# Convolution's closing norms moved into other buffers, three of its output products held back, and a feed-forward tile finished one product later

## The chip, the cores and the metric

One core of one Trainium2 chip runs the whole kernel. The metric is the device time of one launch in microseconds (us). The engines are TensorE (PE), VectorE (DVE), ScalarE (ACT), GpSimd (POOL) and SyncE (SP); each works through its own instructions in their fixed order, and an instruction that waits holds up all that stand behind it on that engine. DMA transfers are issued from the queue of an engine.

## The reference, cut to what matters

One layer of a decoder trunk runs on 528 prompt tokens (16 of them learned meta tokens) and on 8 sequences of 4 new tokens, each with 4096 cached positions in pages:

```python
h = x + 0.5 * swiglu(rmsnorm(x, ffn1_norm), ...)            # FF = 2816
n = rmsnorm(h, mix_norm)                                    # D = 1024
q_lat, q_rope, c_kv, k_rope, glu = project_mixers(n, ...)
a = attn_fn(q_lat, q_rope, c_kv, k_rope, w_uv)              # 8 heads, 512 wide
cv, conv_state = conformer_conv(glu, conv_prev, ...)        # 512 channels, 31 taps, LayerNorm, silu
mix = concatenate([rmsnorm(a, attn_grp_norm), rmsnorm(cv, conv_grp_norm)]) @ w_out
h = h + mix
h = h + 0.5 * swiglu(rmsnorm(h, ffn2_norm), ...)
```

All data are float32. A product is made of three one-pass products: every operand is split into a high and a low part.

## The kernel before

**Layout.** Channels lie on partitions and tokens along the free dimension, so a product of 128 output channels is a pair of PSUM tiles of half the tokens each. `mm3` (L367) issues, per block of 128 input channels, six matmuls of 272 or 280 columns.

**Stages.** The first feed-forward (`ffn`, L729) works through 22 tiles in `GROUPS` (8, 7, 7). The first `plain` tiles (5 in the first feed-forward, 4 in the second) use ordinary products; the others use seven products of blocks for eight (`seven_unit`, L676), whose operands `Combos` (L621) makes beside the plain tiles. Then comes the projection of the mixers, next to which the sample attention (`sample_proc`, L1143), the convolution (`conv_proc`, L914) and the prompt attention (`prompt_worker`, L1327) run. After them come 16 output products: eight of the convolution's half and eight of the attention's half (`out_half`, L1579), each of which is added to the residual `h` by two DVE additions at L1587. The second feed-forward follows.

**Order.** The order of the program is written by processes that yield estimates of PE time to a small planner (`run`, L408). Of the processes that are ready the one with the lowest number goes first: the sample attention and the norms have 0, the two prompt workers 2, the main process with the products 5. Constants such as `CN_LAT` or `AN_LAT` (L45 to L67) are the latencies that the processes sleep for. The compiler's scheduler then sets the order on each engine from this program and from when buffers come free in its own model.

**Weights.** `w_dma` (L271) loads a block of 128x512 into `wr` (3 buffers) from the queue of SP; `w_split` (L289) copies it to `wh` on ACT (L302) and subtracts to `wl` on POOL (L304), or on DVE for the tiles in `prepared`. In the stages of the mixers the load of block j+2 follows the split of block j, and takes the buffer of block j-1, which that block's subtraction on POOL must have read.

**Pages.** `load_chunk` (L1021) loads a chunk of the cache, eight DMAs of 256 KB each from SP's queue; 32 chunks in all. A chunk has four tiles with the tag "y" (8 buffers) or "w" (4 buffers; every third chunk up to chunk `LAST_W` = 30). `chunk_pv` (L1089) of chunk `LAST_W` sets `w_free`. The main process waits for `conv_done` and for `w_free` (L1589, L1590), loads the residual back into the "w" buffers (L1593), and then starts the output products.

**The convolution's end.** `conv_tail` (L964) subtracts the mean (L971), squares the four channel blocks (L542, tag "t" of the pool `tmp`, 10 buffers, which the prompt workers use for their probabilities and their transposes), sums the squares over channels with small matmuls (L453), takes the reciprocal root (`rsqrt` L448: the root on ACT at L485, the rest on DVE), scales, applies tanh (L986, tag "t" too), squares again, takes the second norm, scales (L905) and splits into high and low (L910 on ACT, L911 on POOL).

**The attention's norm.** `attn_norm` (L1565) waits for both prompt workers and the sample attention, squares the attention's output (L542), sums, takes the root, scales (L905) and splits (L910, L911 on DVE). The attention's eight products wait for it.

**The handover in a feed-forward.** When the last plain tile is done, its `evict` (L772) multiplies the four PSUM halves by the norm (L185), applies Silu (L778), multiplies, and splits; then the first `seven_unit` starts. It snapshots its PSUM tiles on ACT (L695). The last three splits of `Combos` (`last`, L672, at L635 on DVE) stand in the last quarter of that plain tile.

Of the kernel before, what the change touches and what calls it, by code (L numbers as in the profile page):

```python
# [50 lines left out]
US_LAT = 4.96  # L51
UP_LAT = 0.5
CS_LAT = 1.73
CN_LAT = 8.16
AN_LAT = 3.71
TAP_PACE = 1.05
CN_WAIT = 8.0
# [8 lines left out]
PAGE_LAT = 2.04  # L66
WEIGHT_TIME = 0.0  # L67

LAST_W = 30


STEPS = "q0k1plr23ue4567"
# [39 lines left out]
def kernel(  # L112
# [45 lines left out]
    def Tm(shape=None, name="t"):  # L158
        return tmp.tile(shape or [128, T], F32, tag="t", bufs=10, name=name)
# [111 lines left out]
    def w_dma(upto):  # L271
        while st["dma"] < min(upto, len(subs)):
            i, c0, n = subs[st["dma"]]
            if n == 0:
                if c0 == 0:
                    raws[i, "a"] = []
                    for kh in range(2):
                        t = U("y" if i in first_new else "x", [128, 2, 512], F32, "ra")
                        nc.sync.dma_start(out=t, in_=stream[i][0][:, 1024 * kh:1024 * kh + 1024])
                        raws[i, "a"].append(t)  # L280
                st["dma"] += 1
                continue
            t = wpool.tile([128, n], F32, tag="wr", bufs=3, name="wr")
            nc.sync.dma_start(out=t, in_=stream[i][0][:, c0:c0 + n])
            raws[st["dma"]] = t
            dma_free[0] = max(dma_free[0], clock[0]) + n * WEIGHT_TIME
            st["dma"] += 1

    def w_split(upto):  # L289
        while st["split"] < min(upto, len(subs)):  # L290
            j = st["split"]
            n = subs[j][2]
            w_dma(j + 1)
            if n == 0:
                splits[j] = seven(*subs[j][0:2])
                st["split"] += 1
                w_dma(j + 8)
                continue
            raw = raws.pop(j)
            hi = wpool.tile([128, n], F32R, tag="wh", bufs=3, name="wh")  # L300
            lo = wpool.tile([128, n], F32R, tag="wl", bufs=3, name="wl")
            nc.scalar.activation(out=hi, in_=raw, func=AF.Copy)  # L302
            eng = nc.vector if subs[j][0] in prepared else nc.gpsimd
            last_lo[0] = eng.tensor_tensor(out=lo, in0=raw, in1=hi.bitcast(F32), op=ALU.subtract)  # L304
            splits[j] = (hi, lo)
            st["split"] += 1

            w_dma(j + (3 if subs[j][0] in mixers else 4))

    def seven(i, m):  # L310
# [134 lines left out]
    last_sum = [None]  # L445
    last_lo = [None]

    def rsqrt(ssums, oi, q, t0=0, site=0, scale=1.0, times=1.0):  # L448

        p1 = SS([128, q], "p1", "nr")  # L450
        for i, ssum in enumerate(ssums):
            for j in range(4):
                nc.tensor.matmul(  # L453
                    out=p1[32 * j:32 * j + 32, :], lhsT=ones_c[:, 0:32], rhs=ssum[:, t0 + q * j:t0 + q * j + q],
                    start=(i == 0), stop=(i == len(ssums) - 1), tile_position=(0, 32 * j),
                )
        scale *= (0.5, 2.0, 1.0)[oi]
        r = tmp.tile([128, 3, q], F32, tag="r", bufs=1, name="r")
        r0, r1, rx = (r[:, i] for i in range(3))
        if times != 1.0:  # L460
            newton3(p1, r0, r1, rx, scale, times)
        else:
            newton(p1, r0, r1, scale)

        nc.vector.tensor_copy(out=r1.bitcast(F32R), in_=r0)
        rr = tmp.tile([128, q], F32R, tag="rr", bufs=1, name="rr")
        last_rsqrt[0] = nc.vector.scalar_tensor_tensor(out=rr, in0=r1, scalar=lowm[:, 0:1], in1=r0, op0=ALU.mult, op1=ALU.add)
        return rr
# [68 lines left out]
        spawn(norm(), 0)  # L537
        return ev

    def square(part, after=None):  # L540
        sq = Tm([128, part.shape[-1]], "sq")
        behind(nc.scalar.activation(out=sq, in_=part, func=AF.Square), after)  # L542
        return sq

# [184 lines left out]
    def ffn(xs, hook, tail=None, plain=NF):  # L729
        ev = Evict(xs.ev, 1)  # L730
        n = xs.n // 2
        cb = steps = None
        f_all = 0

        while turn[0] != "mm" or turn[-1] == "mm":
            turn.append(turn.pop(0))
        for gi, nf in enumerate(GROUPS):
            hid = []
            for f in range(nf):
                f_all += 1  # L740
                if f_all > plain:
                    yield from ev.drain()
                    xs.x = None
                    yield from seven_unit(Weights(), cb, n, hid)
                    continue
                gu = []
                w = Weights()
                pair = [MF()]
                for kh in range(2):
                    for j in range(2):  # L750
                        if len(pair) == j:
                            yield from ev.room()
                            pair.append(MF())
                        for k in range(4 * kh, 4 * kh + 4):
                            mm3(pair[j], *w.at(1024 * kh + 512 * j + 128 * (k % 4)), xs.x[k][:, 0], xs.x[k][:, 1], n,
                                k == 0, k == KD - 1)
                            yield 0.715
                            ev.flush()
                            if plain < NF and xs.ev.ready:
                                if cb is None:  # L760
                                    cb = Combos(xs)
                                    steps = cb.steps()
                                if k % 3 < 2 and (step := next(steps, None)) is not None:
                                    step()
                                if f_all == plain and kh == 1 and j == 1 and k < 7:
                                    cb.last(k - 3, "x")
                        w.done(1024 * kh + 512 * j)
                    if f_all == plain:
                        for k in range(4 * kh, 4 * kh + 4):
                            xs.x[k] = None  # L770

                def evict(pair=pair, gu=gu, w=w):  # L772
                    for j in range(2):
                        t = Tm([128, 2 * n], "gu")
                        halves(lambda *a: behind(v_mul(*a), last_sum[0] if w.i + 1 in first_new else None),
                               t, pair[j], xs.ev.val, n=n)
                        if j == 0:
                            last_silu[0] = nc.scalar.activation(out=t, in_=t, func=AF.Silu)  # L778
                        gu.append(t)
                    x = U("y", [128, 2, 2 * n], F32R, "hid")  # L780
                    hv = Tm([128, 2 * n], "hv")
                    nc.vector.tensor_tensor(out=hv, in0=gu[0], in1=gu[1], op=ALU.mult)
                    nc.scalar.activation(out=x[:, 0], in_=hv, func=AF.Copy)
                    eng = nc.vector if w.i in prepared else nc.gpsimd
                    eng.tensor_tensor(out=x[:, 1], in0=hv, in1=x[:, 0].bitcast(F32), op=ALU.subtract)
                    hid.append(x)
                ev.add(evict)
            yield from ev.drain()
            if gi == len(GROUPS) - 1:
                xs.x = cb = None  # L790
# [173 lines left out]
    def conv_tail():  # L964
# [7 lines left out]
            yield 0.48  # L972
            yield Sleep(1.5)
        csum[0] = None
        s = [square(acc(ct)) for ct in range(4)]
        yield Sleep(CN_LAT)
        ev = Ev()
        yield from rsqrt_proc(lambda: s, 2, ev, site=4)
        s = []
        yield Sleep(1.0)  # L980
        for ct in range(4):
            a = acc(ct)
            nc.vector.scalar_tensor_tensor(out=a, in0=a, scalar=col(P_LG + ct), in1=ev.val, op0=ALU.mult, op1=ALU.mult)

            t = Tm([128, NQ], "th")
            nc.scalar.activation(out=t, in_=a, func=AF.Tanh, scale=0.5, bias=hlb[:, ct:ct + 1])  # L986
            nc.vector.tensor_scalar(out=a, in0=a, scalar1=col(P_LB + ct), scalar2=None, op0=ALU.add)
            nc.vector.scalar_tensor_tensor(out=a, in0=t, scalar=1.0, in1=a, op0=ALU.add, op1=ALU.mult)
            s.append(square(a))
            yield Sleep(0.8)  # L990
        yield Sleep(CN_LAT)
        ev = Ev()
        yield from rsqrt_proc(lambda: s, 2, ev, site=5, scale=0.25, times=0.5)
        s = None
        yield Sleep(1.0)
        for ct in range(4):
            t = scaled(acc(ct), P_CG + ct, ev.val, Tm([128, NQ], "cg"))
            if ct % 2 == 1:
                acc2[ct // 2] = None
            conv_out[ct] = split(t, nc.gpsimd, "x" if ct == 2 else "z")  # L1000
            yield Sleep(0.8)
        conv_done.set(None, 2.0)

# [341 lines left out]
    def main():  # L1345
# [245 lines left out]
        for j in range(4):  # L1591
            hs[j] = U("w", [128, 2, NQ], F32, "h")
            nc.sync.dma_start(out=hs[j], in_=hscr[:, 2 * j:2 * j + 2, :])  # L1593
        for d in range(KD):
            yield from out_half(conv_out)
        yield a_ev
        f2 = Split(P_F2, NQ)
# [211 lines left out]
```

## Time and profile before

| | |
|---|---|
| median of 3 runs | 1177.47 us (1176.39 to 1177.81) |
| the profiled execution | 1183.17 us |
| its span on the core | 1181.4 us |
| PE busy | 1129.1 us, 96% of the span |
| DVE, ACT, POOL busy | 780.1, 537.2, 333.8 us |

A row of a timeline gives the start and the duration in us, the engine and line, the operation, what it writes and reads, how many instructions are merged, and in brackets how long the engine had been idle and what released it. A busy PE is not PE at its peak: the ends of matmuls are modelled. `PEclk` is the granted clock of TensorE as a share of 2.4 GHz.

### The profile page before, as it was taken

To read this page: it belongs to the slowest core of one execution; us is meant where nothing else is said; L and a number is where in the kernel's file an instruction comes from. 1 tells how busy PE (TensorE), PEld (TensorE's weight loads), DVE (VectorE), ACT (ScalarE), POOL (GpSimd) and SP (SyncE) were. 2 spreads that over 40 slices of the span, in tenths; PEclk is the share of its full clock that TensorE was granted. 3 is DMA by queue.
4 is the path that set the end of the run, shared out by engine and by line. 5 is a ranking of instruction groups with operands and counts; after the bars stand their busy time and mean duration, and the time that the engine had idled before them with its cause. 6 is when DMAs were issued, how large, how long until landed. Compare 5 with 4: busy or idle time off the path is not lost.

```text
span 1181.4 us, 24527 instructions
## 1 busy us (share of the span) xinstructions
PE 1129.1 (96%) x9312; PEld 1029.9 (87%) x9312; DVE 780.1 (66%) x1566; ACT 537.2 (45%) x1120; POOL 333.8 (28%) x344
## 2 busy tenths in 40 slices
PE   8999999999999999998899988899999999999995
PEld 8999999999999987876555546899899999999995
DVE  5987158825884447989777357469881489258834
ACT  5545235523555314533544446255552356235642
POOL 4101310042004645676434402342014100410060
PEclk9999999999999989999889999899999999999998
DMA  5243323232226647989779972223333232323222
GB/s 170 68 156 99 85 67 106 85 117 81 92 72 212 220 149 240 272 285 287 220 236 371 351 237 77 72 89 105 102 116 99 72 100 86 115 77 105 70 70 77
DMA packets 91062, 168.60 MB, mean 143 GB/s; under 512 B 18976, under 2 KB 25120, under 8 KB 90944
## 3 DMA queue, kind: packets, MB, share of 16 engines
q1 hardware_dynamic: 88352, 162.27, 42.8%
q0 software_dynamic: 2048, 4.20, 1.2%
q8 instruction: 74, 1.21, 0.4%
q10 hardware_dynamic: 544, 0.56, 0.1%
q14 instruction: 44, 0.36, 0.1%
HBM read 161.33 MB, written 5.65 MB: 141 GB/s over the span
## 4 chain that ended last, share of the span: by engine, by line
PE 83%; DVE 8%; ACT 3%; DMA 2%; issue 2%; POOL 1%; SPq 0%; DVEq 0%; ACTq 0%; POOLq 0%
PE mm L371 40%; PE mm L688 31%; PE sc L1075 3%; PE ob L1097 2%; DVE cacc L947 2%; PE po L1322 2%; PE s L1266 1%; PE mm L1639 1%; PE pt L1306 1%; DMA out<-glu 1%; DMA page<-in_pool_c 1%; DVE xc L635 1%; DMA wr<-in_f_gu 1%; DVE wl L319 1%; DMA wr<-in_w_out_t 0%
## 5 line engine op out<-in xcount | busy, mean ns | idle before, releaser
L304 POOL TENSOR_TENSOR wl<-wr,wh 128x512 fp32r<-128x512 f32 (+1 forms) x157 | 198.2, 1266 | 653.6 <-ACT wh L302 589.6
L688 PE MATMUL mm<-xc,wh 128*128 128x272 f32 (+1 forms) x1960 | 373.8, 291 | 3.4 <-ACT sn L695 3.3
L688 PEld LDWEIGHTS mm<-xc,wh 128*128 128x128 f32 x1960 | 307.8, 189 | 4.5 <-ACT sn L695 3.7
L688 PE MATMUL mm<-xc,wl 128*128 128x272 f32 (+1 forms) x980 | 282.0, 293 | 0.8 <-DVE wl L319 0.8
L371 PE MATMUL mm<-hid,wh 128*128 128x280 f32 (+1 forms) x1352 | 226.7, 289 | 0.0
L302 ACT ACTIVATE wh<-wr 128x512 fp32r<-128x512 f32 (+1 forms) x177 | 108.0, 612 | 260.4 <-PE mm L371 195.8
L371 PEld LDWEIGHTS mm<-hid,wh 128*128 128x128 f32 x1352 | 192.5, 188 | 0.0
L688 PEld LDWEIGHTS mm<-xc,wl 128*128 128x128 f32 x980 | 183.0, 189 | 6.7 <-DVE wl L319 6.7
L371 PE MATMUL mm<-xs,wh 128*128 128x280 f32 (+2 forms) x992 | 176.4, 298 | 4.1 <-ACT wh L302 1.5
L371 PEld LDWEIGHTS mm<-xs,wh 128*128 128x128 f32 (+1 forms) x992 | 146.5, 192 | 8.5 <-issue 2.7
L812 DVE SCALAR_TENSOR_TENSOR h<-mm,h 128x280 f32<-128x280 f32 (+1 forms) x92 | 36.8, 441 | 162.1 <-PE mm L371 162.1
L371 PE MATMUL mm<-hid,wl 128*128 128x280 f32 (+1 forms) x676 | 141.1, 290 | 0.0
L317 ACT ACTIVATE wh<-ra 128x512 fp32r<-128x512 f32 x140 | 87.9, 630 | 71.9 <-PE mm L688 61.8
L371 PE MATMUL mm<-xs,wl 128*128 128x280 f32 (+2 forms) x496 | 111.4, 299 | 2.6 <-POOL glu L888 1.7
L371 PEld LDWEIGHTS mm<-hid,wl 128*128 128x128 f32 x676 | 106.4, 188 | 0.0
L317 ACT ACTIVATE wh<-ws 128x512 fp32r<-128x512 f32 x105 | 66.2, 630 | 83.8 <-DVE ws L329 44.1
L319 DVE TENSOR_TENSOR wl<-ra,wh 128x512 fp32r<-128x512 f32 x140 | 96.3, 689 | 5.6 <-ACT wh L317 2.4
L319 DVE TENSOR_TENSOR wl<-ws,wh 128x512 fp32r<-128x512 f32 x105 | 72.5, 691 | 28.6 <-ACT wh L317 25.8
L947 DVE SCALAR_TENSOR_TENSOR cacc<-glu,par,cacc 128x512 f32<-128x512 f32 x120 | 89.8, 749 | 1.3
L371 PEld LDWEIGHTS mm<-xs,wl 128*128 128x128 f32 (+1 forms) x496 | 80.9, 191 | 6.2 <-issue 2.3
L1028 POOL DMA_INDIRECT rope<-in_pool_r,pr_sb x64 | 63.5, 991 | 54.0 <-PE sc L1075 41.9
L695 ACT ACTIVATE sn<-mm 128x272 f32<-128x272 f32 (+1 forms) x105 | 40.7, 389 | 27.4 <-PE mm L688 27.3
(252 smaller groups left out, 1499.0 us busy)
## 6 DMA issues: line engine op xcount, KB each, us to landing
page<-in_pool_c SPq DMA_DIRECT2D x256, 256.0 KB, 5.3
ra<-in_f_gu SPq DMA_DIRECT2D x70, 512.0 KB, 4.0
wr<-in_f_d SPq DMA_DIRECT2D x62, 256.0 KB, 2.7
wr<-in_f_gu SPq DMA_DIRECT2D x36, 256.0 KB, 3.0
wr<-in_w_in_t SPq DMA_DIRECT2D x24, 256.0 KB, 5.3
wr<-in_f_d SPq DMA_DIRECT2D x30, 192.0 KB, 2.4
wr<-in_w_out_t SPq DMA_DIRECT2D x16, 256.0 KB, 3.0
h<-in_x_t SPq DMA_DIRECT2D x8, 280.0 KB, 6.5
```

The lines of the kernel that those rows point to most:

```text
L302: nc.scalar.activation(out=hi, in_=raw, func=AF.Copy)
L304: last_lo[0] = eng.tensor_tensor(out=lo, in0=raw, in1=hi.bitcast(F32), op=ALU.subtract)
L317: nc.scalar.activation(out=hi, in_=w, func=AF.Copy)
L319: ins = nc.vector.tensor_tensor(out=lo, in0=w, in1=hi.bitcast(F32), op=ALU.subtract)
L371: nc.tensor.matmul(out=ps[a][:m, 0:n], lhsT=w, rhs=x[:, a * n:(a + 1) * n], start=first and o == 0 and j == 0, stop=last and o == 1,)
L688: nc.tensor.matmul(out=ps, lhsT=w_[:, c], rhs=x, start=first and k == 0 and j == 0, stop=k == 3 and j == 2, skip_group_check=True)
L695: nc.scalar.activation(out=s, in_=src, func=AF.Copy)
L812: last = halves(lambda o, i, x: nc.vector.scalar_tensor_tensor(out=o, in0=i, scalar=0.5, in1=x, op0=ALU.mult, op1=ALU.add), hk(d), ps, hk( ...
L947: last_tap = nc.vector.scalar_tensor_tensor(out=ps, in0=g[:, tp:S0 + tp], scalar=w, in1=ps, op0=ALU.mult, op1=ALU.add)
L1028: last = nc.gpsimd.indirect_dma_start(out=rope[:, pg], out_offset=None, in_=pool_r, in_offset=bass.IndirectOffsetOnAxis(ap=pr_sb[:, 32 * g ...
L1075: nc.tensor.matmul(out=ps[32 * b:32 * b + 32], lhsT=w[:, g, 32 * b:32 * b + 32], rhs=x, start=(i_ == 0), stop=(i_ == 2), tile_position=(0, ...
L1097: nc.tensor.matmul(out=ob[32 * b:32 * b + 32, :], lhsT=pts[:, 128 * pg + 32 * b:128 * pg + 32 * b + 32], rhs=tiles[b][:, pg, 0:256], start ...
```

## The change

1. `conv_tail` squares into buffers with the tag "g" (4 buffers, the convolution's own) and issues the sums of each block right behind its square, into a PSUM tile that it holds; tanh goes to "g" as well and is squared in place; the last scaling is in place, without a tile "t". Two of the four outputs take buffers "x" in place of one.
2. `w_dma` issues the weights of the mixers (projections, latents and output, 49 blocks) from ACT's queue.
3. `LAST_W` goes from 30 to 27: chunk 30 takes "y" buffers, and the "w" buffers are free after chunk 27.
4. Before the convolution's sixth output product (`HELD` = 5) the main process waits for the prompt workers and the sample attention, so that three products are left for the time of the attention's norm.
5. In both feed-forwards the `evict` of the last plain tile follows the first product (and a quarter of the second) of the first `seven_unit`; two of the last splits of `Combos` come about a quarter of a tile earlier, the third behind that `evict`. An order that held the `evict` behind the sums of the block weights is dropped.

```diff
-CN_LAT = 8.16
+SQ_LAT = 1.2
+SW_LAT = 3.4
-LAST_W = 30
+LAST_W = 27
+HELD = 5
...
-            nc.sync.dma_start(out=t, in_=stream[i][0][:, c0:c0 + n])
+            (nc.scalar if i in mixers else nc.sync).dma_start(out=t, in_=stream[i][0][:, c0:c0 + n])
...
-                    yield from seven_unit(Weights(), cb, n, hid)
+                    unit = seven_unit(Weights(), cb, n, hid)
+                    if held:
+                        for _ in range(5):
+                            yield next(unit)
+                        held.pop()()
+                        cb.last(3, "x")
+                    yield from unit
...
-                                if f_all == plain and kh == 1 and j == 1 and k < 7:
-                                    cb.last(k - 3, "x")
+                                if f_all == plain and kh == 1 and j == 0 and k in (5, 6):
+                                    cb.last(k - 4, "x")
...
-                        halves(lambda *a: behind(v_mul(*a), last_sum[0] if w.i + 1 in first_new else None),
-                               t, pair[j], xs.ev.val, n=n)
+                        halves(v_mul, t, pair[j], xs.ev.val, n=n)
...
-                ev.add(evict)
+                if f_all == plain < NF:
+                    held.append(evict)
+                else:
+                    ev.add(evict)
...
-        s = [square(acc(ct)) for ct in range(4)]
-        yield Sleep(CN_LAT)
+        p1 = SS([128, NQ // 4], "p1", "nr")
+        for ct in range(4):
+            sq = square(acc(ct), None, "g")
+            yield Sleep(SQ_LAT)
+            column_sums(p1, sq, NQ // 4, ct == 0, ct == 3)
+            sq = None
+            yield 0.25
         ev = Ev()
-        yield from rsqrt_proc(lambda: s, 2, ev, site=4)
+        yield from rsqrt_proc(lambda: p1, 2, ev, site=4)
...
-            t = Tm([128, NQ], "th")
+            t = U("g", [128, NQ], F32, "th")
...
-            s.append(square(a))
-            yield Sleep(0.8)
-        yield Sleep(CN_LAT)
+            nc.scalar.activation(out=t, in_=a, func=AF.Square)
+            yield Sleep(SW_LAT)
+            column_sums(p1, t, NQ // 4, ct == 0, ct == 3)
+            t = None
+            yield 0.25
...
-            t = scaled(acc(ct), P_CG + ct, ev.val, Tm([128, NQ], "cg"))
+            conv_out[ct] = split(scaled(acc(ct), P_CG + ct, ev.val), nc.gpsimd, "x" if ct in (1, 2) else "z")
...
         for d in range(KD):
+            if d == HELD:
+                for e in p_done + [s_done]:
+                    yield e
             yield from out_half(conv_out)
```

`column_sums` holds the four matmuls that stood in `rsqrt`, which now also takes a PSUM tile that is already summed.

## Rows read from the trace of the kernel before

**Rows 1.** Busy engines and the chain that ended last, from the page.

```profile
PE 1129.1 (96%) x9312; PEld 1029.9 (87%) x9312; DVE 780.1 (66%) x1566; ACT 537.2 (45%) x1120; POOL 333.8 (28%) x344
PE 83%; DVE 8%; ACT 3%; DMA 2%; issue 2%; POOL 1%; SPq 0%; DVEq 0%; ACTq 0%; POOLq 0%
```

**Rows 2.** Windows: us, busy of each engine (count), granted clock, DMA share, GB/s.

```profile
641.00:685.00 44.00, 39.56 (x446) 23.16 (x448) 21.35 (x90) 24.79 (x83) 17.65 (x32) 1.00 0.94 330
685.00:728.00 43.00, 40.30 (x465) 23.18 (x460) 25.38 (x88) 22.83 (x74) 3.12 (x10) 0.96 0.56 193
728.00:748.00 20.00, 13.34 (x92) 12.11 (x85) 16.96 (x26) 8.73 (x15) 9.26 (x6) 0.83 0.08 27
748.00:788.00 40.00, 40.00 (x322) 40.00 (x321) 20.56 (x40) 17.64 (x28) 17.70 (x14) 1.00 0.27 85
...
836.00:860.00 24.00, 21.02 (x149) 20.01 (x148) 20.88 (x37) 11.67 (x23) 0.00 (x0) 0.93 0.17 56
```

**Rows 3.** The convolution's end by line, 560 to 790 us (mean, squares, second scaling).

```profile
L971 DVE TENSOR_TENSOR acc<-acc,mu x8: 429/430/438, 637.8 to 640.3; 128x272 f32<-128x272 f32 x8
L542 ACT ACTIVATE sq<-acc x8: 650/666/674, 669.1 to 715.8; 128x544 f32<-128x544 f32 x8
L905 DVE SCALAR_TENSOR_TENSOR cg<-acc,par,rb x4: 779/783/1864, 727.3 to 729.4; 128x544 f32<-128x544 f32 x4
```

**Rows 4.** Timeline, 724 to 757 us: the attention's norm and the first output products.

```profile
727.13 0.66 ACT L542 ACTIVATE sq<-at 128x544 f32<-128x544 f32 x1
727.20 1.14 PE L453 MATMUL p<-sq,ones_c 128*32 128x136 f32 x32 [0.42 <-DVE rb L508]
730.17 1.28 ACT L485 ACT_TABLE_LOAD   x1
731.87 1.00 DVE L486 RECIPROCAL r<-r 128x136 f32<-128x136 f32 x1 [0.63 <-ACT r L485]
732.99 0.30 DVE L487 SCALAR_TENSOR_TENSOR r<-p,r 128x136 f32<-128x136 f32 x1
733.96 1.34 DVE L489 SCALAR_TENSOR_TENSOR r<-r 128x136 f32<-128x136 f32 x1
737.03 4.91 DVE L905 SCALAR_TENSOR_TENSOR at<-at,par,rb 128x544 f32<-128x544 f32 x4
742.35 0.82 PE L371 MATMUL mm<-mix,wh 128*128 128x272 f32 x2 [4.04 <-DVE h L1587]
743.26 2.62 DVE L911 TENSOR_TENSOR mix<-at,mix 128x544 fp32r<-128x544 f32 x4
753.70 0.79 DVE L1587 TENSOR_TENSOR h<-mm,h 128x272 f32<-128x272 f32 x2 [2.22 <-PE mm L371]
756.72 0.79 DVE L1587 TENSOR_TENSOR h<-mm,h 128x272 f32<-128x272 f32 x2 [2.23 <-PE mm L371]
```

**Rows 5.** All additions to the residual behind the output products, by line.

```profile
L1587 DVE TENSOR_TENSOR h<-mm,h x32: 424/431/442, 741.9 to 787.9; 128x272 f32<-128x272 f32 x32
```

**Rows 6.** Timeline, 680 to 686 us: the stall behind the first norm's root.

```profile
684.64 1.07 PE L1097 MATMUL ob<-page,pts 128*32 128x256 f32 x16 [3.21 <-ACT pts L1086]
```

**Rows 7.** Timelines at the two handovers: 79 to 82 us and 836 to 846 us.

```profile
81.75 0.53 PE L688 MATMUL mm<-xc,wh 128*128 128x280 f32 x2 [0.78 <-ACT sn L695]
...
841.57 0.67 ACT L695 ACTIVATE sn<-mm 128x272 f32<-128x272 f32 x2
842.00 0.52 PE L688 MATMUL mm<-xc,wh 128*128 128x272 f32 x2 [2.49 <-ACT sn L695]
```

**Rows 8.** Timelines near 580 and 1171 us: a weight block that lands late; a DMA issued from ACT.

```profile
581.33 0.63 ACT L302 ACTIVATE wh<-wr 128x512 fp32r<-128x512 f32 x1 [4.11 <-DMA wr<-in_w_out_t]
582.65 1.08 PE L1075 MATMUL sc<-rope,qbd 128*32 128x256 f32 x8 [4.28 <-ACT pts L1086]
...
1170.71 0.42 ACTq L1664 DMA_DIRECT2D out<-y  x1
```

**Rows 9.** Waits of SP's queue, 400 to 770 us: us in total, times, longest.

```profile
SPq L284 <- POOL wl L304: 80.4, 20, 27.3
```

More of the change, by code (lines that the diff above doesn't have):

```diff
@@ L446, with column_sums @@
     last_lo = [None]
-    def rsqrt(ssums, oi, q, t0=0, site=0, scale=1.0, times=1.0):
[L450 to L456, printed above, removed]
+    def column_sums(p1, ssum, q, first, last, t0=0):
+        for j in range(4):
+            nc.tensor.matmul(
+                out=p1[32 * j:32 * j + 32, :], lhsT=ones_c[:, 0:32], rhs=ssum[:, t0 + q * j:t0 + q * j + q],
+                start=first, stop=last, tile_position=(0, 32 * j),
+            )
+    def rsqrt(ssums, oi, q, t0=0, site=0, scale=1.0, times=1.0):
+        if isinstance(ssums, list):
+            p1 = SS([128, q], "p1", "nr")
+            for i, ssum in enumerate(ssums):
+                column_sums(p1, ssum, q, i == 0, i == len(ssums) - 1, t0)
+        else:
+            p1 = ssums
         scale *= (0.5, 2.0, 1.0)[oi]
@@ L538, in rsqrt_after, with square @@
         return ev
-    def square(part, after=None):
-        sq = Tm([128, part.shape[-1]], "sq")
+    def square(part, after=None, home="t"):
+        sq = Tm([128, part.shape[-1]], "sq") if home == "t" else U(home, [128, part.shape[-1]], F32, "sq")
         behind(nc.scalar.activation(out=sq, in_=part, func=AF.Square), after)
@@ L732, in ffn @@
         cb = steps = None
+        held = []
         f_all = 0
@@ L786, in evict @@
                     hid.append(x)
-                ev.add(evict)
+                if f_all == plain < NF:
+                    held.append(evict)
+                else:
+                    ev.add(evict)
             yield from ev.drain()
@@ L974, in conv_tail @@
         csum[0] = None
-        s = [square(acc(ct)) for ct in range(4)]
-        yield Sleep(CN_LAT)
+        p1 = SS([128, NQ // 4], "p1", "nr")
[5 more added lines that the diff above has]
+            yield 0.25
         ev = Ev()
-        yield from rsqrt_proc(lambda: s, 2, ev, site=4)
-        s = []
+        yield from rsqrt_proc(lambda: p1, 2, ev, site=4)
+        p1 = None
         yield Sleep(1.0)
+        p1 = SS([128, NQ // 4], "p1", "nr")
         for ct in range(4):
@@ L988, in conv_tail @@
             nc.vector.scalar_tensor_tensor(out=a, in0=t, scalar=1.0, in1=a, op0=ALU.add, op1=ALU.mult)
-            s.append(square(a))
-            yield Sleep(0.8)
-        yield Sleep(CN_LAT)
+            nc.scalar.activation(out=t, in_=a, func=AF.Square)
[3 more added lines that the diff above has]
+            yield 0.25
         ev = Ev()
-        yield from rsqrt_proc(lambda: s, 2, ev, site=5, scale=0.25, times=0.5)
-        s = None
+        yield from rsqrt_proc(lambda: p1, 2, ev, site=5, scale=0.25, times=0.5)
+        p1 = None
         yield Sleep(1.0)
         for ct in range(4):
-            t = scaled(acc(ct), P_CG + ct, ev.val, Tm([128, NQ], "cg"))
+            conv_out[ct] = split(scaled(acc(ct), P_CG + ct, ev.val), nc.gpsimd, "x" if ct in (1, 2) else "z")
             if ct % 2 == 1:
                 acc2[ct // 2] = None
-            conv_out[ct] = split(t, nc.gpsimd, "x" if ct == 2 else "z")
             yield Sleep(0.8)
```

## Prediction

> **What bounds the kernel now.** I read the page first: PE is busy for 96% of the span and the chain that ended last is PE's for 83% [rows 1]. So only what keeps PE waiting, or slow, can be won. The windows by stage come next [rows 2]. Between 748 and 788 us, when the output products run undisturbed, PE issues 322 matmuls in 40 us, or 8.05 per us, at the full clock. Between 728 and 748 us it issues 92 where 161 would fit, and the granted clock averages 0.83. The attention's stretch before it, 641 to 728 us, shows PE nearly always busy, but its weight loads fill only about half of it: many small matmuls, whose recorded ends hide some room. The pages keep the DMA engines at a share of 0.94 up to 685 us and of 0.56 after it.
>
> The rows by line then tell why the poor stretch is there. The convolution's mean is subtracted by 640.7 us, but its squares start at 669.1 us, and its last scaling at 727.3 us [rows 3]: 28 us pass before tiles "t", which the prompt workers also use, are got. So all 16 output products start after the attention has ended, and the convolution's end meets the attention's norm on ACT, DVE and POOL. The timeline shows the meeting [rows 4]: the sums of the attention's squares end at 728.3 us (727.20 + 1.14), the root's table load starts only at 730.17, one Newton step of DVE takes 1.34 us where its like takes 0.30, and PE waits 4.04 us until 742.35 for the residual's additions, which stand behind four scalings of 4.91 us together.
>
> **The change, step by step.** The sum is made against the profiled execution, 1183.2 us; the median shown, 1177.5, is 5.7 us lower, and I take 5.7 off at the end.
>
> *From the attention's end to the last output product.* Before: from 728.3 to about 787.5 us (the last addition starts at 787.9, its first half some 0.4 us sooner [rows 5]), 59.2 us. A product takes 3.02 us (753.70 to 756.72 [rows 4]), 16 take 48.3, so 10.9 us are lost. After: five of the convolution's products are done earlier, three are held, so 11 x 3.02 = 33.2 us follow. The norm must hide behind the three held ones, 9.1 us. From the end of its sums to its first scaling it took 8.69 us (728.34 to 737.03); without the 1.83 us in which ACT was elsewhere and the 1.04 us that the slow Newton step lost, 5.8. First scaling 0.78, split on ACT 0.66 (as a square of this size), subtraction 0.66 (2.62 / 4) [rows 3, 4]: 7.9 us to the first operand. That is inside 9.1. Each further operand costs DVE 1.44 us while a quarter of a product takes 0.75, so the fourth is there at 12.2 and wanted at 11.3: 0.9 us of waiting. With 2 us for late residual additions and the clock I count 3.0 lost in place of 10.9. Together 59.2 - 36.2 = **-23.0 us**; bounds -26.0 (nothing lost) and -15.1 (all 10.9 lost again).
>
> The DVE scalings in this stretch lasted 4.91 us for four, against 0.78 each for their like [rows 3, 4]; POOL was splitting then. The Trainium skill (SBUF — State Buffer, "Who interferes with whom") says that a DVE instruction with two SBUF inputs and a POOL instruction that reads SBUF lock each other out for a whole instruction. That speaks against holding products here, as each brings a weight split to POOL; by it the norm keeps its slow scalings and the sum comes out some 1.8 us later (4.91 - 4 x 0.78).
>
> *Five products moved into the attention.* 15.1 us of PE work is laid into 685 to 728 us. Idle there on record: 43.0 - 40.3 = 2.7 us, and the clock of 0.96 costs 1.7 [rows 2], so the attention's end moves by 15.1 - 4.4 = 10.7. If the room is as large as the weight loads say (23.2 of 43.0 us, where dense products fill theirs), the stretch is 0; with no room at all it is 15.1. I take the recorded idle: **+10.7**.
>
> *The convolution's end moved forward.* By the program's own estimates it takes 38 us (sums of squares 5.8, root 5.3 twice, four blocks of 3.65, scalings and pauses 7.2), so it ends near 679 us, before chunk 27 frees the "w" buffers. In the stretch that it enters, ACT is busy for 24.8 and DVE for 21.4 of 44 us [rows 2], so its work fits; but the root's change of tables on ACT stalled PE by 3.21 us [rows 6], and there the pages set the pace and a loss may not be made good. I take half, **+1.5**; bounds -3.2 (the stall is gone from where it was and costs nothing where it goes) and +3.2. Its sums are issued singly and wait on PE, in front of the sample's scores, for one square of 0.66 us at a time: within these bounds.
>
> *Pages and residual.* Chunks 30 and 31 wait one chunk longer for their buffers, and the residual's four loads move ahead of them on SP. The DMA engines have room after 685 us (share 0.56 [rows 2]): 0, at worst +2.
>
> *The handovers.* In the second feed-forward PE waits 2.49 us for a snapshot that stands on ACT behind the tile's Silu [rows 7], and the clock then averages 0.93 over 24 us [rows 2], 1.7 us more; in the first it waits 0.78 us. The held `evict` takes Silu out of the way. DVE has as much to do as before, and is late next: 20.9 of 24 us [rows 2]. I take half, **-2.5**; bounds 0 and -5.0.
>
> *Weights from ACT's queue.* A block that landed late held ACT, and so PE, for 4.28 us [rows 8]; it stood on SP among page loads. 49 blocks at 0.42 us an issue [rows 8] put 20.6 us on ACT over some 370 us, most of it beside waits. I take **-1.0**; bounds -4.3 and, as a rival below, a loss. The Trainium skill (DMA: Bandwidth & Descriptors, "Issuing engines are not separate DMA queues") says that all queues run on the same 16 engines and that another issuer saves issue time only; by it this term is 0, and the sum 1.0 us later.
>
> Sum: -23.0 + 10.7 + 1.5 + 0 - 2.5 - 1.0 = -14.3, so 1168.9 for an execution like the profiled one and **1163.2 us** for the median.
>
> **The rivals.**
> - *The attention has real room.* If the stretch is 2.7 us in place of 10.7, the time is 1155. For it: half-empty weight loads [rows 2], and the prompt workers get tiles "t" back that the convolution held. Against: PE waits inside chains of dependent steps there, which do not shorten.
> - *The convolution's end is still late*, as ACT and DVE serve the attention first. Then all 16 products follow the attention, but the norm hides behind them: 48.3 + 3.0 in place of 59.2, -7.9. With +3.2 for the disturbed stretch and -3.5 for the last two terms: 1169. For it: 28 us of delay before [rows 3]; against: the cause named is the buffers, and they are changed.
> - *PSUM.* A product holds two of the four banks that the prompt workers use, until its residual has landed. If each holds the workers up for its own length again, the stretch is 2 x 15.1 - 4.4 = 25.8 and the time 1178: no change.
> - *Slower: ACT blocked by its own loads.* A load waits for the buffer that POOL's subtraction must free. SP stood 80.4 us in 20 such waits, up to 27.3 [rows 9]; SP could afford it. If a third of it falls on ACT when PE needs exponentials or copies, that is +26.8 and 1190. It decides from 14.3 us, 18% of the wait. For it: ACT is in order. Against: the load taken is two blocks ahead, so its buffer is mostly free by then.
>
> **How the numbers follow.** Forecast 0.45, room 0.18, late end 0.15, PSUM 0.10, ACT blocked 0.12. The likeliest case alone spans 1158 to 1169. The range, 1152 to 1178, takes in the first three rivals and leaves out the blocked ACT. A measurement of this kernel can tell about 0.2% (2.4 us) from no change. Faster: 0.45 + 0.18 + 0.15 and a third of PSUM, 0.81; same 0.06; slower 0.13.
>
> **What would show it.** Right: squares of the convolution at 641 to 650 us, its last split before 690; five pairs of residual additions before the attention's last square; PE without a wait over 2 us from there on; 8 products behind the held three; the wait of 2.49 us at the second handover below 1. Wrong: the attention's last square later than 742 us (stretch over 15), waits of ACT's queue for POOL's subtractions of more than 10 us in all, or a PE wait for the residual's additions that is back at 4 us.

## The result and the profile after

| | before | after |
|---|---|---|
| median of 6 runs | 1177.64 us (1176.39 to 1183.99) | 1172.16 us (1170.65 to 1175.68) |
| profiled execution, span | 1183.17, 1181.4 us | 1171.67, 1169.9 us |
| mean granted clock in it | 0.978 | 0.988 |

The ratio on record is 0.9934, 95% interval 0.9911 to 0.9956: 7.8 us faster. It is not the quotient of the two medians above, which differ by 5.5 us (0.9953); that lies within the interval. The forecast, 14.3 us faster at 1163.2, had the direction; the size came out at 0.54 of it by the ratio and 0.38 by the medians. The busy row and the chain of the page, against [rows 1]:

```profile
PE 1125.1 (96%) x9312; PEld 1020.6 (87%) x9312; DVE 778.0 (67%) x1566; ACT 536.6 (46%) x1120; POOL 334.6 (29%) x344
PE 79%; DVE 10%; DMA 4%; issue 3%; POOL 2%; ACT 2%; SPq 0%; ACTq 0%; DVEq 0%; POOLq 0%
```

Busy shares say nothing here; the stages do. The windows of [rows 2] again, columns as there:

```profile
641.00:685.00 44.00, 40.08 (x464) 22.44 (x456) 32.66 (x103) 27.11 (x81) 19.65 (x29) 0.96 0.93 312
685.00:728.00 43.00, 39.67 (x400) 23.82 (x401) 16.07 (x65) 19.66 (x69) 6.02 (x16) 0.92 0.47 157
728.00:748.00 20.00, 18.82 (x155) 17.48 (x155) 15.63 (x28) 8.31 (x14) 8.63 (x6) 1.00 0.24 67
...
836.00:860.00 24.00, 23.54 (x180) 22.52 (x179) 21.18 (x38) 13.13 (x25) 0.00 (x0) 1.00 0.20 66
```

The poor stretch is gone: 155 matmuls at the full clock between 728 and 748 us, where there were 92 at 0.83. The stretch before it has not gained: 400 matmuls for 465, at 0.92 for 0.96. Next the convolution's end by its tile `acc` (min/median/max ns, first and last start), against [rows 3]:

```profile
L989 DVE TENSOR_TENSOR acc<-acc,mu x8: 431/432/437, 634.0 to 636.4; 128x272 f32<-128x272 f32 x8
L550 ACT ACTIVATE sq<-acc x4: 673/676/677, 636.5 to 638.2; 128x544 f32<-128x544 f32 x4
...
L928 ACT ACTIVATE mix<-acc x4: 652/658/660, 680.6 to 685.1; 128x544 fp32r<-128x544 f32 x4
```

The squares follow the mean at once, and the last split begins at 685.1 us, 41 us ahead of the attention's last square. That is the step that the forecast rested on. But the timeline from 720 us shows the first output product at 721.10 only:

```profile
721.10 0.52 PE L373 MATMUL mm<-mix,wh 128*128 128x272 f32 x2
...
722.90 0.44 DVE L1612 TENSOR_TENSOR h<-mm,h 128x272 f32<-128x272 f32 x1 [3.59 <-PE mm L373]
...
726.65 0.66 ACT L550 ACTIVATE sq<-at 128x544 f32<-128x544 f32 x1
...
728.68 1.28 ACT L493 ACT_TABLE_LOAD   x1
...
729.74 0.44 PE L452 MATMUL p<-sq,ones_c 128*32 128x136 f32 x8
...
732.76 1.30 POOL L307 TENSOR_TENSOR wl<-wr,wh 128x512 fp32r<-128x512 f32 x1 [2.74 <-ACT wh L305]
732.88 1.33 DVE L496 SCALAR_TENSOR_TENSOR r<-r 128x136 f32<-128x136 f32 x1
734.24 0.30 DVE L497 SCALAR_TENSOR_TENSOR r<-r 128x136 f32<-128x136 f32 x1
...
738.08 3.92 DVE L923 SCALAR_TENSOR_TENSOR at<-at,par,rb 128x544 f32<-128x544 f32 x4 [0.22 <-ACT rb L514]
...
742.49 0.49 PE L373 MATMUL mm<-mix,wh 128*128 128x272 f32 x2 [0.73 <-DVE h L1612]
742.62 3.08 DVE L929 TENSOR_TENSOR mix<-at,mix 128x544 fp32r<-128x544 f32 x3
...
746.19 0.49 PE L373 MATMUL mm<-mix,wh 128*128 128x272 f32 x2 [0.45 <-DVE h L1612]
```

One addition to the residual (722.90) comes before the attention's last square (726.65), not five pairs. The norm is no faster than in [rows 4], yet PE stands only 0.73 and 0.45 us. In both kernels the convolution's products run beside the norm. But in [rows 4] the additions of the first two products already stand behind DVE's four scalings, and the third product waits for them; now those of the fourth and fifth do, and the sixth waits. From the end of the last square to the end of the last product it is 49.2 us (727.3 to 776.5), before 59.1 (727.8 to 786.9).

### The profile page after: what moved, and what is told of

Read it like the earlier page. It is cut to its first block, busy times and chain, and to the rows that moved or that the text cites. A ratio compares the mean times of both kernels' runs of the same rounds, so it can differ in the third digit from the quotient of the medians.

```text
span 1169.9 us, 24513 instructions
## 1 busy us (share of the span) xinstructions
PE 1125.1 (96%) x9312; PEld 1020.6 (87%) x9312; DVE 778.0 (67%) x1566; ACT 536.6 (46%) x1120; POOL 334.6 (29%) x344
## 4 chain that ended last, share of the span: by engine, by line
PE 79%; DVE 10%; DMA 4%; issue 3%; POOL 2%; ACT 2%; SPq 0%; ACTq 0%; DVEq 0%; POOLq 0%
PE mm L373 34%; PE mm L696 31%; PE sc L1100 3%; DMA page<-in_pool_c 2%; PE ob L1122 2%; PE po L1347 2%; PE s L1291 1%; DVE xn L656 1%; DVE xt L662 1%; POOL wl L307 1%; DVE xc L643 1%; PE mm L1668 1%; DVE cacc L965 1%; PE pt L1331 1%; DVE gu L187 1%
## 5 line engine op out<-in xcount | busy, mean ns | idle before, releaser
L305 ACT ACTIVATE wh<-wr 128x512 fp32r<-128x512 f32 (+1 forms) x177 | 107.8, 611 | 234.1 <-PE mm L373 197.7
L373 PE MATMUL mm<-xs,wh 128*128 128x280 f32 (+2 forms) x992 | 172.4, 294 | 5.0 <-ACT wh L305 2.0
L373 PEld LDWEIGHTS mm<-xs,wh 128*128 128x128 f32 (+1 forms) x992 | 143.3, 188 | 9.4 <-issue 3.1
L321 DVE TENSOR_TENSOR wl<-ra,wh 128x512 fp32r<-128x512 f32 x140 | 96.1, 689 | 4.4 <-ACT wh L319 1.6
```

What stands on the lines that cost most here:

```text
L321: ins = nc.vector.tensor_tensor(out=lo, in0=w, in1=hi.bitcast(F32), op=ALU.subtract)
L373: nc.tensor.matmul(out=ps[a][:m, 0:n], lhsT=w, rhs=x[:, a * n:(a + 1) * n], start=first and o == 0 and j == 0, stop=last and o == 1,)
```

## The experiments

The change has three parts that can be switched singly: E, the convolution's end with its page buffer; H, the handovers; Q, ACT's queue. The first four runs and two of the last four fill all eight cells. The table has for each run the ratio to before with its interval, and from its trace two stretches in us: *attention* from the end of the mean's last subtraction to the end of the attention's last square, *output* from there to the end of the last output product.

| run | parts | ratio | attention | output |
|---|---|---|---|---|
| before | none | 1 | 87.1 | 59.1 |
| r9 | H | 0.9963 (0.9937 to 0.9989) | 92.3 | 59.4 |
| r10 | Q | 0.9988 (0.9966 to 1.0010) | 84.9 | 58.9 |
| r2 | H, Q | 0.9962 (0.9936 to 0.9988) | 80.6 | 59.8 |
| r1 | E | 0.9938 (0.9914 to 0.9961) | 94.5 | 43.2 |
| r3 | E, H | 0.9945 (0.9923 to 0.9968) | 100.3 | 46.1 |
| r4 | E, Q | 0.9974 (0.9953 to 0.9995) | 91.0 | 45.8 |
| after | E, H, Q | 0.9934 (0.9911 to 0.9956) | 90.5 | 49.2 |
| r12 | E, page buffer 30 | 0.9882 (0.9853 to 0.9912) | 86.4 | 49.1 |
| r11 | E, H, page buffer 30 | 0.9903 (0.9875 to 0.9932) | 96.1 | 49.0 |
| r6 | E, H, Q, page buffer 30 | 0.9899 (0.9871 to 0.9927) | 88.3 | 49.1 |
| r5 | after, no hold | 0.9935 (0.9911 to 0.9960) | 90.4 | 49.2 |
| r7 | after, tiles "t" | 1.0067 (1.0046 to 1.0089) | 86.7 | 65.5 |
| r8 | after, products early | 0.9995 (0.9974 to 1.0016) | 106.2 | 40.0 |

Two such intervals (0.0025 each) put together leave a single pair uncertain by 0.0035, so the parts are read from the means of all pairs that differ in one part; such a mean is still uncertain by 0.0016 to 0.0021. The stretches are of one execution each, and part of them is lost clock (length times what the granted clock lacks of 1): in the attention stretch none in r2, 1.7 us in before, r1 and r12, 3.4 in r3, r4 and r7 and 5.1 in the others; in the output stretch 3.4 in before, r9, r10 and r8, 5.1 in r2, 6.8 in r7 and none in the others. The line of the hold stands in all kernels but before and r10.

**The parts taken singly.** The three edits, shown as undone:

```diff
E  -LAST_W = 27
   +LAST_W = 30    and conv_tail as before
H  -held.append(evict)
   +ev.add(evict)    and the two last() as before
Q  -(nc.scalar if i in mixers else nc.sync).dma_start(out=t, in_=stream[i][0]...
   +nc.sync.dma_start(out=t, in_=stream[i][0]...
```

r1 has H and Q undone. 

> Only the convolution's end is changed (own slots, single sums, hold, last page buffer); the two handovers and the queue of the mixers' weights are as before. Theory A: the early end lets the convolution's products cover the attention's norm, worth 9 to 10 us from the attention's last square to the last product, of which some 3 us are given back ahead of it by a denser stretch 585 to 725 us; the time is 1171 to 1173 (ratio 0.995). Rival B: the profiled execution of before (mean clock 0.978, 5.5 us above its median) was a poor one there, the end is worth under 3 us and the handovers and the queue made the gain; the time is 1175 to 1178 (ratio 0.998 to 1.000).

r2 has E undone. 

> The changed kernel with the old end of the convolution (tiles t, sums together, last page buffer 30); handovers and queue stay changed. Theory A: the convolution's squares start at 665 to 672 us and its last split ends after 725 us again, the output products start after 728 us with a gap of some 4 us, the time is 1174 to 1176, 3 us below before (the handovers' 3.7 us of the profiles, less what part of them is luck). Rival B: 1171 to 1173, as fast as the whole change.

r3 has Q undone. 

> The changed kernel with the mixers' weights back on SP's queue. Theory A: the wait of 4.28 us of PE for a weight block on ACT near 580 us is back or one like it is, and the time is 0 to 2 us longer than the changed kernel's, 1172 to 1174. Rival C (a price of the queue: 49 issues of 0.42 us on ACT, in front of the attention's exponentials): 1168 to 1170, since the 3 us that the profiles give back between 585 and 725 us were the queue's.

r4 has H undone. 

> The changed kernel with the old end of the plain tiles (eviction before the first product of the seven). Theory A: the wait of PE for the snapshot at the handover into the seven is back with 2 to 3 us in the second feed-forward and about 0.8 in the first, the milestones of the profiles (2.3 and 1.4 us) are lost, time 1174 to 1176. Rival D: only the wait of 2.49 us in the second is lost, and the 2.3 us of the first were run-to-run clock: 1172.5 to 1173.5.

r9 is the kernel before with H alone. 

> The kernel before with the two handovers changed and nothing else. Theory A: the wait of 2.49 us for the snapshot becomes one of 1.2 us for the weight's first half on ACT, as in the changed kernel (1.19), and 0.6 us is won at the first handover, so 2 us in all, ratio 0.998. Rival D: the fewer low-clock stretches beside the handovers (1.7 us each in two profiles of three) come with it, 4 to 5 us, ratio 0.996, as the run with the handovers undone (0.9974 against 0.9934) says.

r10 is the kernel before with Q alone. 

> The kernel before with the mixers' weights issued from ACT's queue and nothing else. Theory A: the wait of 3.7 to 4.3 us of PE near 576 us is gone, yet the time is the same within 2 us (ratio 0.998 to 1.002), since the pages on the same 16 DMA engines pace that stretch. Rival C: the issues on ACT cost more than the wait, 3 to 4 us slower (ratio 1.003), as the pair with and without the queue beside the new end alone suggests (0.9974 against 0.9938). Rival I: the wait's 4 us are won, ratio 0.9965.

*E*: its four pairs (r1 to before, r3 to r9, r4 to r10, after to r2) give -0.0062, -0.0018, -0.0014, -0.0028, on average -0.0031 or 3.6 us. Rival B fell with r1 and r2. In the four pairs the output stretch is 10.6 to 15.9 us shorter and the attention stretch 6.1 to 9.9 us longer. Of the other runs here, r3, r4 and r10 came out in time as theory A had them; r9 came out at rival D's 0.996, but its interval takes in theory A's 0.998.

*H*: -0.0037 (r9), -0.0026, +0.0007, -0.0040 and, with page buffer 30, +0.0021 (r12 to r11): on average -0.0015 or 1.8 us, which is not clear of nothing (uncertain by 0.0016). In the traces the 0.78 us at the first handover are gone in after and still there in r4, and at the second the wait of [rows 7] is there in all five kernels without H (2.46 to 2.50 us) and in none of the nine with it; another has half its place. It reads so in r9, and 1.19 us again in after:

```profile
838.36 0.52 PE L697 MATMUL mm<-xc,wh 128*128 128x272 f32 x2 [1.19 <-ACT wh L320]
```

The weight's first half on ACT is late now. From the last output product to the second feed-forward's first addition it takes 102.4 to 102.5 us in all nine with H, and 103.8, 103.7, 102.4, 103.9 and 104.0 without it. The four long ones have 1.7 us of lost clock in that stretch; without that they are no longer than the others. r4 has the wait without the lost clock, and 102.4 us like those with H. So what H wins there, 1.1 us on average, is the clock, and the wait itself was worth nothing.

*Q*: -0.0012 (r10), +0.0036, -0.0001, -0.0011, -0.0004 (r11 to r6): +0.0002 on average, nothing within 2 us. Yet the wait is Q's to take: near 576 us PE stands 3.6 to 4.3 us in all six kernels without Q, as in r3, and in none of the eight with it:

```profile
580.29 0.66 PE L1100 MATMUL sc<-rope,qbd 128*32 128x256 f32 x8 [4.10 <-ACT pts L1111]
```

In r4 and r10 (Q without H) another of 4.80 us stands at 552 us instead. ACT's waits for weight blocks between 400 and 770 us, before (L302) and after (L305):

```profile
ACT wh L302 <- DMA wr<-in_w_in_t: 17.1, 5, 4.6
ACT wh L302 <- DMA wr<-in_w_out_t: 4.1, 1, 4.1
```

```profile
ACT wh L305 <- DMA wr<-in_w_in_t: 3.8, 4, 2.1
ACT wh L305 <- DMA wr<-in_w_out_t: 0.9, 1, 0.9
```

21.2 us of waiting became 4.7, and the time is the same. The pages keep the DMA engines at a share of 0.82 (before) and 0.88 (after) from 560 to 641 us; that they set the pace there is argued from it, not tried by itself.

ACT got other waits for these. A load now stands in ACT's own queue until POOL's subtraction has freed its buffer. Such a stretch of after, rows of ACT and POOL only:

```profile
513.85 0.63 ACT L305 ACTIVATE wh<-wr 128x512 fp32r<-128x512 f32 x1 [1.84 <-PE mm L373]
...
516.64 1.27 POOL L307 TENSOR_TENSOR wl<-wr,wh 128x512 fp32r<-128x512 f32 x1
...
517.94 1.62 ACTq L287 DMA_DIRECT2D wr<-in_w_in_t  x2
...
519.59 1.28 ACT L493 ACT_TABLE_LOAD   x1 [5.11 <-POOL wl L307]
```

ACT does nothing from 514.48 us, and its first load goes out 0.03 us after POOL's subtraction ends (517.91). Between 400 and 770 us ACT stands 35 us in this way in after, in front of 27 of 45 loads, and 30 to 37 us in all eight kernels with Q. The list of ACT's waits puts only 5.5 us down to these subtractions, since it gives a whole wait to what ended last. In all, ACT is busy for 159 of these 370 us before and for 165 after.

**The hold.** r5 takes it out:

```diff
-HELD = 5
+HELD = 8
```

> The changed kernel with the hold set to 8 of 8 products, so none is held. Theory A: the hold never decides, because the order written at build time puts the convolution's products behind the attention anyway; the products start at 716 to 722 us and the time is the changed kernel's, 1170 to 1174. Rival E: the hold is what keeps products for the norm; without it five or more products run ahead of the attention's last square and PE waits over 4 us for the norm's scalings, 1176 to 1180.

Theory A held: 0.9935 against 0.9934. The two traces have the same 9312 matmuls, 1566, 1120 and 344 instructions of DVE, ACT and POOL in the same order. So the hold changes nothing. The reason is read from the program: the estimates by which it is written out put the convolution's end behind the attention's, so no product is there yet that the hold could stop. r8, which shortens them, bears it out: its first product starts at 704.7 us.

**The products laid into the attention**, as the forecast assumed. r8 shortens those estimates, so that the first five stand ahead of the attention's end:

```diff
-SQ_LAT = 1.2
-SW_LAT = 3.4
+SQ_LAT = 0.3
+SW_LAT = 0.4
-        yield Sleep(RS_LAT)
+        yield Sleep(1.0 if site in (4, 5) else RS_LAT)
...
-conv_done.set(None, 2.0)
+conv_done.set(None, 0.0)
```

> The changed kernel with shorter estimates for the convolution's end in the build-time order (1.2, 3.4, 4.05 and 1.0 us become 0.3, 0.4, 1.0 and 0), so that five products are written ahead of the attention's end and three behind it, as the prediction assumed. Theory A: PE is full there, so the attention's last square moves from 727 to 737 to 742 us; three held products (9.1 us) do not cover the 15 us from the last square to the first split operand, PE waits 4 us or more, and the time is 2 to 5 us longer than the changed kernel's, 1174 to 1177. Rival H (the forecast's terms): the norm shortens to 8 us and hides behind the three, the recorded idle takes in 4 us of the five products, the time is 1166 to 1170.

1180.01 us, more than theory A expected: 7 us slower than after. Five pairs of additions now come before the attention's last square, as forecast. Against after, the attention stretch grows by 15.7 us and the output stretch shrinks by 9.2. Rows of its timeline:

```profile
741.20 0.64 ACT L550 ACTIVATE sq<-at 128x544 f32<-128x544 f32 x1
...
752.27 3.26 DVE L923 SCALAR_TENSOR_TENSOR at<-at,par,rb 128x544 f32<-128x544 f32 x4
...
754.18 1.27 PE L373 MATMUL mm<-mix,wh 128*128 128x272 f32 x4 [2.88 <-ACT mix L928]
```

The scalings start 10.4 us behind the end of the last square (741.84), what is left of the convolution's products does not reach that far, and PE stands 2.88 us. PE's time in the attention is not free, and products spent there are missing as cover.

**The slots.** r7 puts the tiles "t" back and keeps the single sums:

```diff
-            sq = square(acc(ct), None, "g")
+            sq = square(acc(ct))
-            t = U("g", [128, NQ], F32, "th")
+            t = Tm([128, NQ], "th")
```

> The changed kernel with the squares and the tanh of the convolution's end back in tiles t, still summed one by one. Theory A: the slots are what brought the end forward; the squares start after 660 us, the last split ends after 715 us, products start after 722 us, the time is 1174 to 1176. Rival G: summing one by one is enough, as one tile t at a time is got soon; squares start at 636 to 645 us, the last split ends before 700, and the time is the changed kernel's, 1171 to 1174.

1185.9 us, 10 us worse than theory A: slower than before. Its squares by their tile, then PE's long waits in its timeline:

```profile
L550 ACT ACTIVATE sq<-acc x4: 646/650/653, 668.7 to 677.7; 128x544 f32<-128x544 f32 x4
```

```profile
729.24 0.48 PE L512 MATMUL p<-rr,unit 2*128 2x136 f32 x2 [4.61 <-DVE rr L475]
...
746.14 0.82 PE L373 MATMUL mm<-mix,wh 128*128 128x272 f32 x2 [4.05 <-DVE h L1612]
```

The squares are at 668.7 us again, as in [rows 3]. So the wait was for the tiles, which the forecast named. Rival G fell. That it is slower even than before is not taken apart: r7 also has the page buffer at 27, which costs some 5 us below, and sums one by one, each block waiting for its own tile. What its trace shows is that the second norm's root now meets the attention's end, and PE waits for both.

**The page buffer.** r6 gives the third page buffer back to chunks 28 to 30; r11 and r12 do so without Q, and without H and Q:

```diff
-LAST_W = 27
+LAST_W = 30
```

> The changed kernel with the third page buffer kept to chunk 30 instead of 27. Theory A: with 27 the pages of chunk 30 are issued at 690.7 us, behind the chunk before, and its scores run at 700 to 705 us; with 30 they are issued at about 682, the scores of chunk 30 end by 698, the attention's last square comes at 718 to 723 us in place of 727, and the residual still lands before the attention's end, so the time is 3 to 6 us below the changed kernel's, 1166 to 1169. Rival F: PE is full from 688 us on, so pages landing sooner bring nothing; the last square stays at 725 to 728 us and the residual's loads, issued after 700 us, hold the first products: 1172 to 1175.

> The changed kernel with the third page buffer kept to chunk 30 and the weights back on SP's queue. Theory A: queue worth 0 to 2 us of loss or gain, so 1167 to 1171 (ratio 0.989 to 0.992), like the kernel with chunk 30 alone. Rival C: without the issues on ACT 3 us faster, 1164 to 1167 (0.987).

> The kernel before with the new end of the convolution alone and the third page buffer as before (30). Theory A: the end alone with chunk 27 came to 0.9938; with chunk 30 it is 2 to 4 us better, ratio 0.990 to 0.992, 1168 to 1171, and the attention's last square comes 83 to 88 us behind the mean's subtraction in place of 94.5. Rival F: the page buffer brings nothing without the other parts, ratio 0.993 to 0.995.

All three are faster than their partners: -0.0035 (r6 to after), -0.0042 (r11 to r3), -0.0056 (r12 to r1), on average -0.0044 or 5.2 us. SP's rows and PE's scores of chunk 30 (in after the last ten of its 16 matmuls), first after, then r6:

```profile
676.70 4.49 SPq L1066 DMA_DIRECT2D page<-in_pool_c  x8
682.19 1.88 SPq L1618 DMA_DIRECT2D h<-hscr  x4
690.72 13.36 SPq L1066 DMA_DIRECT2D page<-in_pool_c  x16
...
704.37 1.05 PE L1100 MATMUL sc<-page,qlat 128*32 128x256 f32 x10
```

```profile
678.92 18.50 SPq L1066 DMA_DIRECT2D page<-in_pool_c  x24
709.86 1.76 SPq L1618 DMA_DIRECT2D h<-hscr  x4
...
703.19 1.05 PE L1100 MATMUL sc<-page,qlat 128*32 128x256 f32 x16
```

In after, no page goes out between 681.2 and 690.72 us; the next one leaves as chunk 28's products end and free their buffer. With 30 the pages follow each other, and the residual, loaded at 709.9, still comes before the first product. The single traces show less of the gain: the two stretches together are 2.3 (r6), 1.3 (r11) and 2.2 us (r12) shorter. In r6 theory A had the time right and the way not: it had the attention's last square at 718 to 723 us; it stayed at 727, as its mean's subtraction was 2.2 us later and PE is nearly full there. Between 2 and 5 us is what these runs support. With 30, E is worth -0.0118, -0.0060 and -0.0063 (r12 to before, r11 to r9, r6 to r2), 9.5 us on average. r11 came out as theory A had it; r12 came out a little better than theory A's 0.990 to 0.992. **r12, the new end alone with the page buffer left as it was, is the fastest point measured**, 1168.21 us against 1179.59 of before; r6 and r11 lie within its interval.

## Why the prediction was right, and where it was not

*From the attention's end to the last product, and five products moved* (-23.0 + 10.7 = -12.3 together). The cause was right: tiles "t" held the end back (r7), and with it early the two chains no longer meet. The output stretch fell by 9.9 us and the attention stretch grew by 3.4, so the sum of the two terms was not far off. Its two halves were, and that they made up for each other is luck: only the first product began inside the attention, and the arrangement forecast, when r8 had it, was 7 us slower than after. The other products follow the attention, as in the rival that had the norm hidden behind them, though that rival's reason, a late end, was wrong. The diff's hold was read as what it does; which way the order would be written out was not asked. Where the products do go in (r8), the room assumed is not there: the attention stretch grew by 15.7 us, beyond the bound of 15.1. That also ends the rival with real room.

*The norm.* 7.9 us from the end of its sums to the first operand was too short: from 730.2 us to the end of the first subtraction (743.3) it is 13.2 us. The slow Newton step stayed (732.88), and on DVE all four scalings and a residual addition stand before the first subtraction, where the sum had one scaling. The Trainium skill (SBUF — State Buffer, "Who interferes with whom") says that a DVE instruction with two SBUF inputs and a POOL instruction that reads SBUF shut each other out; the trace agrees, with 1.33 us for a Newton step beside POOL's split and 0.30 for its like after it, and 3.92 us for the four scalings. That costs almost nothing here, since five products (728.0 to 745.7 us) run beside the norm; behind three, as forecast, PE waits 2.88 us (r8).

*The convolution's end moved forward* (+1.5, bounds -3.2 to +3.2). With the page buffer left alone the attention stretch changes by -0.7, +3.8 and +7.7 us (r12, r11, r6 to before, r9, r2): 3.6 on average, over the upper bound. But 5.1 of the 7.7 are clock that r6's execution lost and r2's did not; without them the average is 1.9, close to the forecast. The stall of 3.21 us [rows 6] has become three of 1.72, 1.14 and 1.49 us behind the second scaling.

***Pages and residual* (0, at worst +2) is the term that failed.** The prediction said that the DMA engines have room after 685 us. They have (share 0.47), but what was missing was a buffer: from the residual's loads (684.07) to the next page 6.6 us pass. It cost 2 by the traces and 5 us by the timing.

*The handovers* (-2.5): 1.8 us by five pairs, not clear of nothing; 1.1 are seen in the traces, as clock beside the second wait. That wait is 1.19 us and not below 1: next late was ACT's weight half, not DVE.

*Weights from ACT's queue* (-1.0): 0. The Trainium skill (DMA: Bandwidth & Descriptors, "Issuing engines are not separate DMA queues") had it so, and the runs agree: the time stayed, though the waits for weight blocks went. The rival in which ACT is blocked by its loads had the wait right and its price wrong. ACT stands 35 us for POOL's subtractions, more than the 26.8 that the rival put down and than the 10 that the prediction named as a sign of being wrong. The argument against it, that a load two blocks ahead finds its buffer free, failed for 27 loads of 45. No time was lost that five pairs can show: ACT is idle for over 200 of those 370 us in either kernel.

By the runs the sum is -9.5 (end) + 5.2 (page buffer) - 1.8 + 0 = -6.1 us, against -7.8 measured and -14.3 forecast. PSUM was not tried by itself.

## What to carry to other kernels

Work that only has to be done before a join is best kept for the latency behind the join: as cover it is worth its whole length there, and in a stage that is already full it costs that length. Ask of each buffer that a change takes over what it was pacing, even where the resource that it feeds has room. A wait that goes from the trace is a gain only if what it stood for was the pace of the stage.

## What the runs showed of the hardware

82 runs of the kernel before lie between 1171.7 and 1187.6 us, and their mean granted clock between 0.972 and 0.989. The time falls by 0.89 us for each 0.001 of clock (correlation -0.94); with that taken off, the spread falls from 3.6 to 1.2 us. So the profiled execution of before, at 0.978 and 5.5 us above its median, had lost more clock than most. Two profiles are best compared stretch by stretch with the clock beside them, and a difference of a few us between two of them is not yet the change's.

The mean clock differs between kernels too: 0.980 over the 82 runs of before, 0.986 over six of after and 0.985 over eight of r5, which has the same instructions in the same order. By the slope above that would be 5 of the 7.8 us. But the slope is one within a kernel: Q, added to H, raises the mean clock by 0.005 to 0.006 in three pairs (r9 to r2, r3 to after, r11 to r6) and leaves the time where it is. How much of the change's gain is clock stays open.
